# A two-layer decoder trunk: the first norm's weight applied by features, first loads and first product in another order, last stores in pieces

## The chip, the cores and the metric

The kernel runs on one core of a Trainium2 chip. The core has five engines that run side by side and wait for each other by semaphores: TensorE (PE, with its weight loads as PEld), VectorE (DVE), ScalarE (ACT), GpSimd (POOL) and SyncE (SP), which here only starts transfers. The metric is the device time of one execution in microseconds (us), lower is better.

## What is computed

The input is 256 tokens of 1024 features, float32. Two layers follow, cut here to what the change touches:

```
for l in range(2):
    h = rms_norm(x, attn_norm[l])          # x / sqrt(mean(x^2) + eps) * weight
    proj = h @ w_in[l]                     # 1024 -> 1720, cut into 11 parts
    ... two attention groups, mixed, projected by w_out, added to x
    h = rms_norm(x, mlp_norm[l])
    x = x + square(relu(h @ w_ff1[l])) @ w_ff2[l]
return rms_norm(x, final_norm)
```

The weight of the norm belongs to a feature (a column of x), the root of the mean to a token (a row). A product needs h with the features on the partitions, so h is transposed on TensorE first.

## The kernel before

The 256 tokens are two tiles of 128 (t = 0, 1), the 1024 features two halves of 512 (nb = 0, 1), each of four chunks of 128. Float32 products are made of three matmuls: every operand is split into a rounded part `hi` and a rest `lo`, and `mm3` (L350) adds hi·hi, hi·lo and lo·hi (L352 to L354). The factor 1/sqrt(mean) is not applied to h: it is applied to the results, as `rx`, after the product. So the norm before the product (`norm`, L417) is only x times the weight.

Weights come as one stream of tiles `raw` (512 KB, two chunks of 512 columns), which `ask` (L314) starts on SP's queue in the order in which they are used. ACT rounds each to `whi` (L334, two instructions of 512 columns), DVE or POOL subtracts to `wlo` (L336). `raw` has 6 buffers; the first eight tiles go to DVE.

The first norm: `gain` loads the weight onto all 128 partitions (`partition_broadcast`, 256 KB each half), DVE multiplies (L428), TensorE transposes four blocks into the PSUM tile `tr` (two buffers, L384), ACT rounds them in one instruction of 512 columns (L393), DVE subtracts (L394). The order on TensorE and SP is written by the program itself: chains of work (generators) are run by a small planner, `Driver`, that counts expected TensorE time and the times in `dr.event`, and emits the instructions in the order of its clock. ACT, DVE and POOL are ordered by the scheduler of the framework.

The first product (columns 512 to 1023 of w_in) is made by `proj_both` (L851), which takes two chunks of the weights for tile 0 and then for tile 1, four times over. `kcs_after` takes its result to the keys (`kd`, `kcv`), which are transposed later by `key_chain` (started 3468 ns of the planner's clock later). Before data come, TensorE runs matmuls of zeros (`warm_up`, L298). The last norm is `finish` (L1157): after each part of the last sums ACT squares and adds up (`sumsq`, L376), POOL makes the mean (L414) and its power -0.5 (L1164), ACT and DVE scale one half each (L1167, L1169), and each half leaves in one store of 256 KB, ACT's from ACT's queue, DVE's from SP's.

Of the kernel before, what the change touches and what calls it, by code (L numbers as in the profile page):

```python
# [9 lines left out]
F32 = mybir.dt.float32  # L10
# [6 lines left out]
P = 128  # L17
# [131 lines left out]
def _pack(inp):  # L149
# [11 lines left out]
    arr["cst"] = CONSTANTS  # L161
# [65 lines left out]
def trunk(ctx: ExitStack, tc: tile.TileContext, x, wst, gains, pos, cw2, cst, out):  # L227
# [35 lines left out]
    def gain(l, name, halves=()):  # L263
# [3 lines left out]
        if halves:  # L267
            m = n // len(halves)
            for i, also in enumerate(halves):
                nc.sync.dma_start(t[:, i * m : i * m + m], gains[o + i * m : o + i * m + m].partition_broadcast(P))  # L270
                also()
        else:
            nc.sync.dma_start(t, gains[o : o + n].partition_broadcast(P))
        return t

    idt = const.tile([P, P], F32, name="idt")
# [7 lines left out]
    ident = idt  # L284
# [15 lines left out]
    warm_up(9)  # L300
# [109 lines left out]
    def after_x(t, a, n):  # L410

        ss = sumsq(X[t][:, a : a + n], n)
        r = sm.tile([P, 1], F32, name="mean", bufs=6)
        nc.gpsimd.tensor_scalar(r, ss, 1.0 / D, EPS if a == 0 else mean[t], op0=OP.mult, op1=OP.add)  # L414
        mean[t] = r

    def norm(t, nb, g, hT, tag):  # L417

        yield "event", ("x", t, tag, nb * 512)
        if tag[1] == "mlp":  # L420
            if hT[nb] is None:
                hT[nb] = [hl.tile([P, 2, 2, S], F32R, name=f"hm{nb}{i}", tag="hl") for i in range(2)]
        elif hT[nb] is None:
            hT[nb] = halves_pair(f"h{nb}")
        h = tm.tile([P, 512], F32, name="h", tag="tm")
        n = slice(nb * 512, nb * 512 + 512)
# [3 lines left out]
        c = slice(t * P, (t + 1) * P)  # L430
# [40 lines left out]
    def layer(l, hT):  # L471
# [379 lines left out]
        def proj_both(a, chunks, n, after):  # L851

            accs = []
            w = weights(chunks)
            for c in range(0, chunks, 2):
                pairs = [next(w), next(w)]
                for t in range(NT):
                    if c % 4 == 0:
                        yield "event", a(t)[1] + (c // 4,)
                    if c == 0:  # L860
                        yield "get", "s"
                        accs.append(PS("s")[:, :n])
                    h = a(t)[0]
                    for i, wc in enumerate(pairs):
                        mm3(accs[t], h(c + i), wc, c + i == 0, c + i == chunks - 1)
                    yield "pe", 6 * max(107, n / 2.4), 0
                    if c == chunks - 2:
                        after(t, accs[t])
# [14 lines left out]
        def kcs_after(t, acc):  # L883
# [9 lines left out]
            dr.spawn(1, later(3468, key_chain(kd, t, 0, kc)))  # L893
# [250 lines left out]
    def begin(l, halves=()):  # L1144

        g = gain(l, "attn", halves)
# [10 lines left out]
    def finish(t, g):  # L1157
# [7 lines left out]
        for i, h in enumerate(hs):  # L1165
            if i == 0:
# [3 lines left out]
            (nc.sync if i else nc.scalar).dma_start(out[t * P : (t + 1) * P, i * 512 : i * 512 + 512], h)  # L1170

    def main():
        def load_a():
            nc.sync.dma_start(idt, cst[:, :P])
            load_x(1, 0)
            ask(2)

        def load_b():
            load_x(1, 1)
            ask(5)  # L1180

        def next_x():
            load_a()
            load_x(0, 1)

        load_x(0, 0)
        h = begin(0, (next_x, load_b))
        for t in range(NT):
            for nb in range(2):
                dr.event(("x", t, (0, "attn"), nb * 512), [2000, 5000, 2600, 5500][2 * t + nb])  # L1190
# [3 lines left out]
        nc.sync.dma_start(cs, cst)  # L1194
        nc.vector.tensor_copy(identb, ident)
        nc.scalar.copy(maskb, K("causal"))
        yield "event", ("h", 0, (0, "attn"), 0)
        warm_up(4)
# [25 lines left out]
```

## Time and profile before

| what | us |
|---|---|
| timed runs: lowest, median, highest (3 runs) | 634.9, 637.33, 637.53 |
| the profiled execution: its own time | 635.02 |
| the profiled execution: its span, first to last instruction | 633.2 |
| busy in the span: PE, DVE, ACT, POOL | 615.3, 424.0, 354.6, 305.8 |

The profile is of one execution. Busy PE is counted as the union of matmuls that overlap, so a share of 97% is not TensorE at its peak. Outside the span lie 635.02 - 633.2 = 1.8 us. A wait that the profile names is the last that ended before an instruction began.

### The profile page before, as it was taken

To read this page: it belongs to the slowest core of one execution; us is meant where nothing else is said; L and a number is where in the kernel's file an instruction comes from. 1 tells how busy PE (TensorE), PEld (TensorE's weight loads), DVE (VectorE), ACT (ScalarE), POOL (GpSimd) and SP (SyncE) were. 2 spreads that over 40 slices of the span, in tenths; PEclk is the share of its full clock that TensorE was granted. 3 is DMA by queue.
4 is the path that set the end of the run, shared out by engine and by line. 5 is a ranking of instruction groups with operands and counts; after the bars stand their busy time and mean duration, and the time that the engine had idled before them with its cause. 6 is when DMAs were issued, how large, how long until landed. Compare 5 with 4: busy or idle time off the path is not lost.

```text
span 633.2 us, 9990 instructions
## 1 busy us (share of the span) xinstructions
PE 615.3 (97%) x3587; PEld 518.7 (82%) x3587; DVE 424.0 (67%) x742; ACT 354.6 (56%) x776; POOL 305.8 (48%) x292
## 2 busy tenths in 40 slices
PE   8999899999999999999999899999999999999995
PEld 5788788878888888888888778798888888888885
DVE  5997787686647557467677867866774673765662
ACT  5666757555636446365554476665564564454552
POOL 2184415263545636456466641425553654655451
PEclk9999999999999999999999899999999999999999
DMA  8857612245655654755644665116446565565501
GB/s 310 298 187 259 238 45 90 95 155 183 197 170 176 222 167 167 232 167 197 196 128 137 215 215 204 49 53 178 160 139 223 167 216 179 191 210 169 200 1 66
DMA packets 31729, 108.42 MB, mean 171 GB/s; under 512 B 3776, under 2 KB 4416, under 8 KB 31680
## 3 DMA queue, kind: packets, MB, share of 16 engines
q1 hardware_dynamic: 31392, 107.27, 51.6%
q8 instruction: 28, 0.46, 0.3%
q10 hardware_dynamic: 288, 0.52, 0.2%
q14 instruction: 21, 0.17, 0.1%
HBM read 106.73 MB, written 1.05 MB: 170 GB/s over the span
## 4 chain that ended last, share of the span: by engine, by line
PE 83%; DVE 9%; ACT 3%; DMA 2%; issue 2%; POOL 0%; POOLq 0%; SPq 0%; ACTq 0%; DVEq 0%
PE acc L352 14%; PE acc L353 14%; PE acc L354 14%; PE s L1100 14%; PE s L1101 7%; PE pv L1100 5%; PE tr L384 4%; DVE wlo L336 3%; PE pv L1101 2%; PE pv L721 2%; DMA raw<-in_wst_dram 2%; PE pv L772 2%; DVE h L428 1%; PE acc L962 1%; ACT whi L334 1%
## 5 line engine op out<-in xcount | busy, mean ns | idle before, releaser
L336 POOL TENSOR_TENSOR wlo<-raw,whi 128x512 fp32r<-128x512 f32 (+3 forms) x172 | 249.2, 1472 | 208.8 <-ACT whi L334 208.4
L334 ACT CAST whi<-raw 128x512 fp32r<-128x512 f32 (+2 forms) x360 | 201.6, 610 | 96.8 <-PE acc L354 59.6
L336 DVE TENSOR_TENSOR wlo<-raw,whi 128x512 fp32r<-128x512 f32 (+3 forms) x188 | 162.1, 899 | 53.5 <-ACT whi L334 53.5
L1100 PE MATMUL s<-hm,whi 128*128 128x512 f32 x384 | 141.7, 399 | 0.0
L1101 PE MATMUL s<-hm,wlo 128*128 128x256 f32 x384 | 107.8, 281 | 0.0
L352 PE MATMUL acc<-whi,u 128*128 128x512 f32 (+1 forms) x264 | 101.4, 384 | 0.0
L353 PE MATMUL acc<-wlo,u 128*128 128x512 f32 (+1 forms) x264 | 101.1, 383 | 0.0
L354 PE MATMUL acc<-whi,u 128*128 128x512 f32 (+1 forms) x264 | 101.1, 383 | 0.0
L1100 PEld LDWEIGHTS s<-hm,whi 128*128 128x128 f32 x384 | 72.2, 188 | 17.8
L1101 PEld LDWEIGHTS s<-hm,wlo 128*128 128x128 f32 x384 | 72.5, 189 | 0.2
L354 PEld LDWEIGHTS acc<-whi,u 128*128 128x128 f32 x264 | 49.6, 188 | 9.8
L352 PEld LDWEIGHTS acc<-whi,u 128*128 128x128 f32 x264 | 49.6, 188 | 9.8
L353 PEld LDWEIGHTS acc<-wlo,u 128*128 128x128 f32 x264 | 49.6, 188 | 9.4
L1043 DVE SCALAR_TENSOR_TENSOR x<-acc,r,x 128x512 f32<-128x512 f32 (+1 forms) x33 | 24.1, 731 | 49.4 <-PE acc L354 49.4
L1100 PE MATMUL pv<-hm,whi 128*128 128x512 f32 x128 | 51.0, 399 | 0.0
L352 PE MATMUL acc<-whi,h 128*128 128x512 f32 (+2 forms) x112 | 41.3, 369 | 0.0
L353 PE MATMUL acc<-wlo,h 128*128 128x512 f32 (+2 forms) x112 | 40.2, 359 | 0.2 <-POOL wlo L336 0.2
L354 PE MATMUL acc<-whi,h 128*128 128x512 f32 (+2 forms) x112 | 40.0, 357 | 0.0
L1071 ACT COPY sq<-s 128x256 f32<-128x256 f32 x48 | 17.6, 372 | 39.2 <-PE s L1101 38.6
L659 ACT ACTIVATE p<-s,nm 128x128 f32<-128x128 f32 (+1 forms) x96 | 34.0, 433 | 6.5 <-DVE nm L655 3.9
L1076 ACT CAST u<-sq 128x512 fp32r<-128x512 f32 x32 | 19.8, 619 | 31.2 <-DVE sq L1075 31.2
L1101 PE MATMUL pv<-hm,wlo 128*128 128x256 f32 x128 | 36.0, 281 | 0.0
(192 smaller groups left out, 995.7 us busy)
## 6 DMA issues: line engine op xcount, KB each, us to landing
raw<-in_wst_dram SPq DMA_DIRECT2D x178, 512.0 KB, 4.2
raw<-in_wst_dram SPq DMA_DIRECT2D x8, 416.0 KB, 3.6
raw<-in_wst_dram SPq DMA_DIRECT2D x4, 420.0 KB, 5.0
raw<-in_wst_dram SPq DMA_DIRECT2D x4, 384.0 KB, 3.1
x<-in_x_dram SPq DMA_DIRECT2D x4, 256.0 KB, 5.2
g_mix<-in_gains_dram SPq DMA_DIRECT2D x2, 512.0 KB, 5.8
g_mlp<-in_gains_dram SPq DMA_DIRECT2D x2, 512.0 KB, 5.6
g_attn<-in_gains_dram SPq DMA_DIRECT2D x2, 512.0 KB, 4.4
```

The costliest lines, as they stand in the source:

```text
L334: nc.scalar.copy(hi[:, v], r[:, v])
L336: E(eng).tensor_sub(lo[:, v], r[:, v], hi[:, v].bitcast(F32))
L352: mm(acc, ah, wh, start=start, stop=False, **k)
L353: mm(acc, ah, wl, start=False, stop=False, **k)
L354: mm(acc, al, wh, start=False, stop=stop, **k)
L384: nc.tensor.transpose(tr[:rows, c, :], col, ident)
L659: nc.scalar.activation(p[:, k], s[:, k], AF.Exp, bias=nm[:, a : a + 1], scale=scale)
L1043: nc.vector.scalar_tensor_tensor(X[t][:, c], acc, scale, X[t][:, c], op0=OP.mult, op1=OP.add)
L1071: nc.scalar.copy(low[:, n], acc[:, S:])
L1076: nc.scalar.copy(hi, sq)
L1100: mm(accs[half][j], wh[:, f], h.rearrange("p k n -> p (k n)"), start=c == 0, stop=False)
L1101: mm(accs[half][j][:, :S], wl[:, f], h[:, 0], start=False, stop=c == KC - 1)
```

## The change

The first norm's weight now comes as eight columns beside the identity matrix (feature on the partition, chunk on the column): the constants get a field `gain0`, and one load brings both. The x tiles are transposed as they are; the weight is applied when ACT and DVE take the transposed blocks from PSUM, one instruction for each block of 128, since each block has its own column of the weight. The first loads stand in another order, `proj_both` takes four chunks for a tile before it turns to the other tile, seven and two matmuls of zeros stand where nine and four stood, and the key chains of the first layer start 5500 ns after their product. At the end tile 1 is scaled and stored in four pieces, and the mean of the parts under 512 columns is made by DVE.

```diff
     add("ident", np.eye(P))
+    add("gain0", np.zeros((P, KC)))
...
+    arr["cst"][:, a : a + n] = inp["attn_norm"][0].reshape(KC, P).T
...
-    idt = const.tile([P, P], F32, name="idt")
+    idg = const.tile([P, P + KC], F32, name="idt")
...
-    warm_up(9)
+    warm_up(7)
...
-        nc.gpsimd.tensor_scalar(r, ss, 1.0 / D, EPS if a == 0 else mean[t], op0=OP.mult, op1=OP.add)
+        (nc.vector if n < 512 else nc.gpsimd).tensor_scalar(r, ss, 1.0 / D, EPS if a == 0 else mean[t], op0=OP.mult, op1=OP.add)
...
+        if g is None:
+
+            tr = yield from trans([X[t][:, n][:, j * P : (j + 1) * P] for j in range(4)])
+            hi, lo = (x[:, :, c] for x in hT[nb])
+            gf = idg[:, P + nb * 4 : P + nb * 4 + 4]
+            with urgent():
+                for j in range(4):
+                    nc.scalar.activation(hi[:, j], tr[:, j], AF.Copy, scale=gf[:, j : j + 1])
+                for j in range(4):
+                    nc.vector.scalar_tensor_tensor(lo[:, j], tr[:, j], gf[:, j : j + 1], hi[:, j].bitcast(F32), op0=OP.mult, op1=OP.subtract)
...
-            for c in range(0, chunks, 2):
-                pairs = [next(w), next(w)]
-                for t in range(NT):
+            for t, part in [(0, (0, 4)), (1, (0, 4)), (0, (4, 8)), (1, (4, 8))]:
...
-            dr.spawn(1, later(3468, key_chain(kd, t, 0, kc)))
+            dr.spawn(1, later(3468 if l else 5500, key_chain(kd, t, 0, kc)))
...
-        for i, h in enumerate(hs):
-            if i == 0:
+        for a in range(0, D, 256 if t else 512):
+            n = 256 if t else 512
+            h = hs[a // 512][:, a % 512 : a % 512 + n]
+            if a < 512:
                 nc.scalar.activation(h, h, AF.Copy, scale=v)
             else:
                 nc.vector.tensor_scalar(h, h, v, None, op0=OP.mult)
-            (nc.sync if i else nc.scalar).dma_start(out[t * P : (t + 1) * P, i * 512 : i * 512 + 512], h)
+            (nc.sync if a >= 512 else nc.scalar).dma_start(out[t * P : (t + 1) * P, a : a + n], h)
...
         load_x(0, 0)
-        h = begin(0, (next_x, load_b))
+        nc.sync.dma_start(idg, cst[:, : P + KC])
+        ask(1)
+        load_x(1, 0)
+        ask(2)
+        load_x(0, 1)
+        load_x(1, 1)
+        ask(5)
+        h = begin(0)
...
-        warm_up(4)
```

What stands on SP's queue at the start before: x of tile 0 first half, weight of the norm first half, identity, x of tile 1 first half, two weight tiles, x of tile 0 second half, weight of the norm second half, x of tile 1 second half, three weight tiles. After: x of tile 0, identity with the weight, a weight tile, x of tile 1, a weight tile, x of tile 0 and x of tile 1 second halves, three weight tiles.

TensorE's queue at the start of the program before the change; `h` is x times the weight, `whi_127` the first weight tile, `s_227` and `s_234` the sums of tile 0 and tile 1, and each name of a tile has its buffer number:

```order
L384 MATMUL tr_197<-idt_96,h_193 128x128 x4
L384 MATMUL tr_204<-idt_96,h_195 128x128 x4
L298 LDWEIGHTS zero_102
L298 MATMUL s_211<-zero_102 128x512
...
L352 MATMUL s_227<-whi_127,h00_191 128x512
L353 MATMUL s_227<-wlo_128,h00_191 128x512
L354 MATMUL s_227<-whi_127,h01_192 128x512
...
L352 MATMUL s_234<-whi_127,h00_191 128x512
```

After the change; `x0_94` and `x1_95` are x of tile 0 and 1, `tr_219` is tile 1's first half, `tr_234` tile 0's second, `tr_264` tile 1's second, `s_215` and `s_277` are the sums:

```order
L381 MATMUL tr_166<-idt_96,x0_94 128x128 x4
...
L349 MATMUL s_215<-whi_122,h00_164 128x512
L350 MATMUL s_215<-wlo_123,h00_164 128x512
L351 MATMUL s_215<-whi_122,h01_165 128x512
L381 MATMUL tr_219<-idt_96,x1_95 128x128 x4
L381 MATMUL tr_234<-idt_96,x0_94 128x128 x4
L349 MATMUL s_215<-whi_122,h00_164 128x512
...
L351 MATMUL s_215<-whi_131,h01_165 128x512
L381 MATMUL tr_264<-idt_96,x1_95 128x128 x4
L349 MATMUL s_277<-whi_122,h00_164 128x512
```

Only tile 0's first transposes stand before the first product now; the other three groups have moved in among its matmuls, and tile 1 begins after tile 0's four chunks.

ACT's queue at the start before the change; `junk` is the square for the mean, `h00` and `h10` the rounded halves:

```order
L376 ACTIVATE junk_169,ss_168<-x0_94 128x512
L376 ACTIVATE junk_174,ss_173<-x1_95 128x512
L393 CAST h00_191<-tr_197 128x4x128
L393 CAST h00_191<-tr_204 128x4x128
L334 CAST whi_127<-raw_125 128x512 x2
L334 CAST whi_135<-raw_133 128x512 x2
```

The same place after the change:

```order
L373 ACTIVATE junk_183,ss_182<-x0_94 128x512
L331 CAST whi_122<-raw_120 128x512 x2
L431 ACTIVATE h00_164<-tr_166,idt_96 128x128 x4
L373 ACTIVATE junk_188,ss_187<-x1_95 128x512
L331 CAST whi_131<-raw_129 128x512 x2
L373 ACTIVATE junk_193,ss_192<-x0_94 128x512
L431 ACTIVATE h00_164<-tr_219,idt_96 128x128 x4
L431 ACTIVATE h10_232<-tr_234,idt_96 128x128 x4
```

The first weight tile has moved ahead of the first half of h, and each half of h and tile is four instructions where it was one.

ACT's last instructions, of tile 1, before the change:

```order
L376 ACTIVATE junk_6785,ss_6784<-x1_95 128x256
L1167 ACTIVATE h_5123<-h_5123,rstd_6790 128x512
L1170 DMA out_0_dram<-h_5123 128x512
```

and after it:

```order
L373 ACTIVATE junk_6794,ss_6793<-x1_95 128x256
L1177 ACTIVATE h_5132<-h_5132,rstd_6799 128x256 x2
L1180 DMA out_0_dram<-h_5132 128x256 x2
```

Both scalings stand ahead of both stores.

## Rows read from the trace of the kernel before

**Rows 1.** Windows of first and second product: us, busy PE PEld DVE ACT POOL, clock, DMA

```profile
9.47:23.08 13.61, 12.84 (x57) 9.76 (x57) 11.67 (x22) 10.83 (x23) 3.94 (x6) 1.00 1.03 398
23.08:35.62 12.54, 12.29 (x58) 9.60 (x57) 12.40 (x28) 6.73 (x18) 5.17 (x5) 1.00 0.67 219
```

**Rows 2.** Chain of waits, first 15 us: start, us, what

```profile
1.16 4.09 DMA g_attn<-in_gains_dram
6.10 2.19 PE tr L384 x8
14.23 0.23 PE s L354
```

**Rows 3.** Timeline: start, us, engine, line, operation, count; the second product's first matmul

```profile
23.08 0.39 PE L352 MATMUL acc<-whi,h 128*128 128x512 f32 x1
```

**Rows 4.** DMA view, single issues at 0.72, 1.63, 2.10, 2.57: KB, us to landing

```profile
x<-in_x_dram SPq DMA_DIRECT2D x1, 256.0 KB, 2.7
idt<-in_cst_dram SPq DMA_DIRECT2D x1, 64.0 KB, 4.0
x<-in_x_dram SPq DMA_DIRECT2D x1, 256.0 KB, 4.3
raw<-in_wst_dram SPq DMA_DIRECT2D x1, 512.0 KB, 5.1
```

**Rows 5.** DMA view, 0 to 30 us in 40 slices

```profile
GB/s 0 0 128 369 154 129 277 412 371 410 399 391 240 298 415 415 432 420 419 407 405 392 421 415 389 407 384 395 394 406 407 365 265 262 275 111 244 218 22 0
```

**Rows 6.** Timeline of ACT and DVE, 11 to 31 us: casts, square, instructions of 128 columns

```profile
11.80 0.63 ACT L376 ACTIVATE junk<-x 128x512 bf16<-128x512 f32 x1 [0.20 <-DMA x<-in_x_dram]
13.02 1.14 ACT L334 CAST whi<-raw 128x512 fp32r<-128x512 f32 x2 [0.49 <-DMA raw<-in_wst_dram]
29.36 0.34 DVE L459 SCALAR_TENSOR_TENSOR ra<-s,rx,cs 128x128 f32<-128x128 f32 x1
29.62 0.46 DVE L462 SCALAR_TENSOR_TENSOR rb<-s,rx,cs 128x64 f32<-128x64 f32 x2
30.18 0.37 ACT L881 ACTIVATE kcv<-s,rx 128x128 f32<-128x128 f32 x1 [3.67 <-DVE rb L462]
30.44 0.36 ACT L881 ACTIVATE V<-s,rx 128x128 f32<-128x128 f32 x1
```

**Rows 7.** Groups by line, 3 to 24 us: count, busy us, mean ns, idle before

```profile
L393 ACT CAST h<-tr 128x512 fp32r<-128x512 f32 x4 | 2.3, 586 | 1.3 <-PE tr L384 1.3
```

**Rows 8.** View of line 298, the matmuls of zeros: duration ns min/median/max

```profile
L298 PE MATMUL s<-zero x13: 380/634/634, 1.0 to 9.3; 128*128 128x512 bf16 x13
```

**Rows 9.** Windows and timeline at 355 us, second layer

```profile
355.00:360.00 5.00, 2.90 (x10) 2.79 (x11) 3.81 (x11) 3.07 (x9) 1.35 (x4) 0.74 0.89 323
357.10 0.45 PE L384 MATMUL tr<-idt,kd 128*128 128x128 f32 x2 [2.27 <-DVE kT L509]
```

**Rows 10.** Timeline of POOL and PE at 46 to 55 us

```profile
46.07 1.39 POOL L528 TENSOR_TENSOR FT<-kcT,posl 64x120 f32<-64x120 f32 x2
54.48 0.65 PE L962 MATMUL acc<-raw,FT 128*32 128x128 f32 x16
```

**Rows 11.** Timeline of the end, and a small DVE instruction from 61 us

```profile
627.29 0.42 ACT L376 ACTIVATE junk<-x 128x256 bf16<-128x256 f32 x1 [1.97 <-DVE x L1043]
627.96 0.27 POOL L414 TENSOR_SCALAR mean<-ss,mean 128x1 f32<-128x1 f32 x1 [2.27 <-ACT junk L376]
628.31 0.55 POOL L1164 TENSOR_TENSOR rstd<-mean,mhalf 128x1 f32<-128x1 f32 x1
628.89 0.72 ACT L1167 ACTIVATE h<-h,rstd 128x512 f32<-128x512 f32 x1 [1.10 <-POOL rstd L1164]
629.65 0.34 ACTq L1170 DMA_DIRECT2D out_dram<-h  x1
61.29 0.18 DVE L732 RECIPROCAL wv<-pv 128x4 f32<-128x4 f32 x1
```

**Rows 12.** DMA view, last store: KB, us to landing

```profile
out_dram<-h ACTq DMA_DIRECT2D x1, 256.0 KB, 2.5
```

More of the change, by code (lines that the diff above doesn't have):

```diff
@@ L160, in _pack @@
     arr["cw2"] = np.concatenate([w2k, w2v.reshape(L, P, 128)], 2)
-    arr["cst"] = CONSTANTS
+    arr["cst"] = CONSTANTS.copy()
+    a, n = CST["gain0"]
+    arr["cst"][:, a : a + n] = inp["attn_norm"][0].reshape(KC, P).T
     return {k: np.ascontiguousarray(v) for k, v in arr.items()}
@@ L261, in trunk, with gain @@
     goff = {"attn": (0, 1024), "mix": (1024, 1024), "mlp": (2048, 1024), "lat": (3072, 384)}
-    def gain(l, name, halves=()):
+    def gain(l, name):
         o, n = goff[name] if l < L else (0, 1024)
@@ L266, in gain @@
         t = gp.tile([P, n], F32, name=f"g_{name}", tag="glat" if name == "lat" else "g", bufs=1 if name == "lat" else 2)
[L267 to L273, printed above, removed]
+        nc.sync.dma_start(t, gains[o : o + n].partition_broadcast(P))
         return t
-    idt = const.tile([P, P], F32, name="idt")
+    idg = const.tile([P, P + KC], F32, name="idt")
     cs = const.tile([P, cst.shape[1]], F32, name="cs")
@@ L283, in trunk @@
     ck = lambda name, t, n: K(name)[:, t * n : (t + 1) * n]
-    ident = idt
+    ident = idg[:, :P]
     identb = const.tile([P, P], BF16, name="identb")
@@ L424, in norm @@
             hT[nb] = halves_pair(f"h{nb}")
+        n = slice(nb * 512, nb * 512 + 512)
+        c = slice(t * P, (t + 1) * P)
+        if g is None:
[7 more added lines that the diff above has]
+                    nc.vector.scalar_tensor_tensor(lo[:, j], tr[:, j], gf[:, j : j + 1], hi[:, j].bitcast(F32), op0=OP.mult, op1=OP.subtract)
+            dr.put("tr", 1500)
+            dr.event(("h", t, tag, nb), 1600)
+            return
         h = tm.tile([P, 512], F32, name="h", tag="tm")
-        n = slice(nb * 512, nb * 512 + 512)
         with urgent():
@@ L429, in norm @@
         yield "pe", 0, 700
-        c = slice(t * P, (t + 1) * P)
         cols = [h[:, j * P : (j + 1) * P] for j in range(4)]
@@ L851, in proj_both @@
         def proj_both(a, chunks, n, after):
-            accs = []
-            w = weights(chunks)
-            for c in range(0, chunks, 2):
-                pairs = [next(w), next(w)]
-                for t in range(NT):
[L858 to L868, printed above, removed]
+            src, w, accs = weights(chunks), [], [None, None]
+            for t, part in [(0, (0, 4)), (1, (0, 4)), (0, (4, 8)), (1, (4, 8))]:
+                yield "event", a(t)[1] + (part[0] // 4,)
+                if part[0] == 0:
+                    yield "get", "s"
+                    accs[t] = PS("s")[:, :n]
+                h = a(t)[0]
+                for c in range(*part):
+                    if c == len(w):
+                        w.append(next(src))
+                    mm3(accs[t], h(c), w[c], c == 0, c == chunks - 1)
+                    yield "pe", 3 * max(107, n / 2.4), 0
+                if part[1] == chunks:
+                    after(t, accs[t])
         hin = lambda t: (of_tile(hT, t), ("h", t, tag("attn")))
@@ L1142, in layer, with begin @@
         return hN
-    def begin(l, halves=()):
-        g = gain(l, "attn", halves)
+    def begin(l):
+        g = gain(l, "attn") if l else None
         h = [None, None]
@@ L1169, in finish @@
                 nc.vector.tensor_scalar(h, h, v, None, op0=OP.mult)
-            (nc.sync if i else nc.scalar).dma_start(out[t * P : (t + 1) * P, i * 512 : i * 512 + 512], h)
+            (nc.sync if a >= 512 else nc.scalar).dma_start(out[t * P : (t + 1) * P, a : a + n], h)
     def main():
[L1173 to L1184, printed above, removed]
-        load_x(0, 0)
-        h = begin(0, (next_x, load_b))
+        load_x(0, 0)
+        nc.sync.dma_start(idg, cst[:, : P + KC])
[6 more added lines that the diff above has]
+        h = begin(0)
         for t in range(NT):
             for nb in range(2):
-                dr.event(("x", t, (0, "attn"), nb * 512), [2000, 5000, 2600, 5500][2 * t + nb])
+                dr.event(("x", t, (0, "attn"), nb * 512), [1900, 4300, 3900, 4700][2 * t + nb])
+        nc.sync.dma_start(cs, cst)
+        yield "event", ("h", 0, (0, "attn"), 0)
+        warm_up(2)
         for nb in range(2):
@@ L1193, in main @@
                 after_x(t, nb * 512, 512)
-        nc.sync.dma_start(cs, cst)
         nc.vector.tensor_copy(identb, ident)
         nc.scalar.copy(maskb, K("causal"))
-        yield "event", ("h", 0, (0, "attn"), 0)
-        warm_up(4)
         for l in range(L):
```

## The prediction

> **What bounds the kernel now.** I read the windows by stage first, then the chain of waits at the start, the transfers, and the timeline at both ends. TensorE is the engine that sets the pace: in the first product it is busy 12.84 of 13.61 us, in the second 12.29 of 12.54, while DVE (12.40 of 12.54) runs close behind it in the second [rows 1]. The second product's first matmul starts at 23.08 us [rows 3], and from there TensorE hardly stops for long, so a time won before 23.08 should reach the end of the program if nothing else holds it back. What holds the start is in the chain [rows 2]: a transfer of the norm's weight that lands at 1.16 + 4.09 = 5.25, DVE's multiplication, eight transposes from 6.10 to 8.28, ACT's and DVE's split, and only then, at 9.47, the first real matmul [rows 1]. In 9.47 to 23.08 the 48 matmuls at 0.23 us each [rows 2] make 11.0 us; the other 2.6 are transposes and waits. The edits at the start act on these 23 us, those at the end on the last 6; on the other engines the order in between is nearly untouched.
>
> **The transfers.** x's first half lands at 0.72 + 2.7 = 3.4, the weight of the norm at 5.25, the identity at 1.63 + 4.0 = 5.6, the next x at 6.4, the first weight tile at 2.57 + 5.1 = 7.7 [rows 2, 4]. They land in the order of issue, so 512 KB take 7.67 - 6.40 = 1.27 us, half of it for 256 KB. The weight of the norm took 5.25 - 3.4 = 1.8 us for 256 KB, and while it came the rate fell to 154 and 129 GB/s, against about 400 later [rows 5]. With it gone and the identity next (0.4 us, as from 5.25 to 5.6), I place the landings at 3.8 for identity and gain, 5.1 for the first weight tile, 5.8 for x of tile 1, 7.0 for the second weight tile, 7.7 and 8.3 for the second halves of x, 9.6 and 10.9 for the next weight tiles. The other end: if the low rate is that of a start, and not of this load, everything lands 1.3 later.
>
> **The small instructions.** Removed are four multiplications on DVE, four casts on ACT of 0.59 us [rows 7] and four subtractions on DVE. Added are 16 ACTIVATE and 16 SCALAR_TENSOR_TENSOR of 128 columns. The nearest rows, with a scale from a column too, last 0.37 on ACT and 0.34 on DVE, but the next one starts 0.26 later on both [rows 6]. I take 0.26 each and 0.37 for the last, so 1.15 for a group of four; the other end is 0.37 each, 1.5. The Trainium skill's page "ScalarE: Activation LUTs", section "What ACT_TABLE_LOAD costs", speaks against cutting: an ACTIVATE has 186 ns of its own, 93 more for a scale taken from a column, and neighbours overlap by 93, which gives 293 ns at 128 columns as an estimate against the 260 of the row. By the page the eight that stand on the path below would cost 0.3 us more and the sum would be 632.7; the row decides for me.
>
> **The path to the end of the first product.** ACT works in order, and the new order puts the first weight tile ahead of tile 0's h, so all that follows waits for the landing at 5.1: two casts of the first weight tile, 1.14 [rows 6], from 5.1 to 6.3; four for tile 0's h to 7.4; a square with its readout, about 0.75, to 8.1; two casts of the second tile to 9.2; a square to 9.9; four for tile 1 to 11.0, four for tile 0's second half to 12.1. DVE follows: tile 0's rest 7.2 to 8.3, the second weight tile's rest to about 10.1, tile 1's rest 10.3 to 11.4. TensorE's first real matmul goes at 6.7, when the first rounded block is there. The third waits for DVE to 7.5. Eight transposes stand behind it in the queue; at the 0.27 of the early ones (2.19 for eight [rows 2]) they end near 9.8. All else of TensorE is queued behind them, tile 0's remaining nine matmuls first, and these need the second weight tile's rest anyway (10.1). They end near 12.0. The last four transposes need DVE to have read `tr_219` (11.4), so they wait for nothing more and end at 12.5. Then 36 matmuls at 0.23 make 8.3: the product ends at 20.8, against 23.08. The next weight tiles (9.6, 10.9, cast by 15) are in time. This edit gives 2.3 us. Early end: transposes twice as fast and no wait, 19.6, a gain of 3.5. Late end: the transfers 1.3 later and 8 x 0.11 for the instructions, 23.0, no gain.
>
> **The middle.** The second stage needs 48 x 0.23 = 11.0 us and eight transposes; 1.5 of its 12.54 us are not matmuls [rows 1]. The key chains, started later in the planner's order, should spare some waits; I take 0.2, from 0.6 gained to 0.5 lost, since DVE has 0.14 us free there and must now run 2.3 us earlier. POOL's last additions to `FT` move back in its queue behind two more weight halves, but they end at 47.5 and are wanted at 54.48 [rows 10], so 7 us cover that. The zero matmuls lie in TensorE's waiting time.
>
> **The end.** The mean moves from POOL (0.27) to DVE, where the smallest row is 0.18; I take 0.15 gained with the handover, from -0.2 to 0.3 [rows 11]. Two scalings of 256 columns on ACT, each up to 0.42 where the one took 0.72, cost 0.06 to 0.12. Both stores stand behind both scalings, so the second is issued one issue of 0.34 later, but carries 128 KB less, about 0.33 us. The last store lands 2.5 us after its issue [rows 12]. Together 0.1 gained, from 0.5 lost to 0.5 gained. The Trainium skill's page "DMA: Bandwidth & Descriptors", section "Anatomy of one DMA — SWDGE (gpsimd) path", has a rule against more and smaller stores: about 2.0 us of a transfer are fixed and only bytes/436e3 scale. By it, halving saves 0.30, less than the second issue costs, and the end would come out even. The last store's 2.5 us [rows 12] agree with the 2.6 that the page gives for 256 KB, as an estimate.
>
> **The sum.** 2.3 + 0.2 + 0.1 = 2.6. Against the profiled execution's 635.02 that is 632.4. The timed runs are 634.9, 637.33 and 637.53, so the profiled one lies with the lowest, 2.3 below the median. Nothing in the change shows which level the median of new runs takes: 632.4 or 637.33 - 2.6 = 634.7. I take the middle, 633.5.
>
> **Rivals.**
> 1. TensorE's clock eats part of it. The zero matmuls took 634 ns at first and 380 at the last [rows 8], that is 1.2 GHz and then 2.4, after near continuous work from 6.1. At 355 us the granted clock of the stretch is 0.74, after an idle time of 2.27 us [rows 9]. Now TensorE's early work is broken by waits between 6 and 12 us. If the rise comes only a quarter into the dense 36 matmuls, nine of them last 0.2 longer (512 columns at 1.2 in place of 2.4 GHz), 1.8: a gain of 0.8, 634.2 on the profiled level, 636.5 on the median's. For: fewer zero matmuls. Against: five unbroken us from 0.97. Chance 0.2.
> 2. The removed load wasn't what slowed the transfers, and the landings stay 1.3 later: gain 1.3, so 633.7 or 636.0. For: only one such stretch at the very start. Against: the rate falls again (240, 298) when the second half of that weight comes [rows 5]. Chance 0.1.
> 3. Slower: the clock stays at 1.2 GHz through the whole first product, because TensorE never gets a stretch without a wait. Each 512-column matmul then costs 0.2 more; 48 make 9.6, so 635.02 - 2.6 + 9.6 = 642.0. It decides from 13 matmuls on against no gain, from 29 on against 0.5% slower. Against: after 12 us, 36 matmuls stand without a wait between them. Chance 0.06.
> 4. More than forecast: 3.5 at the start and 0.6 in the middle, 630.9 to 633. Chance 0.1.
>
> **How the numbers follow.** The forecast has 0.54. About 0.5% (3.2 us) is what a measurement of this kernel can tell from no change. Against the median of 637.33, faster means below 634.1: some two thirds of the forecast's chance (0.37), nearly all of rival 4 (0.1), a little of rivals 1 and 2 (0.05): 0.52. Slower by more than 3.2 is rival 3: 0.06. The rest, 0.42, is within. The range goes from 630.5 (rival 4 on the lower level) to 637.0 (rivals 1 and 2 on the upper level, with some loss in the middle); the forecast's own is 632.0 to 635.2.
>
> **What would show it.** Right: the first weight tile lands near 5.1, the first real matmul starts near 6.7, the second product's first near 20.8, and every stage after it lies 2 to 3 us earlier with the same lengths. Wrong: a landing after 6; matmuls of 512 columns 0.43 apart after 12 us; a second product longer than 12.5; the last store landing more than 4.9 us after the last square starts (629.65 + 2.5 - 627.29 before [rows 11, 12]). The forecast fails most easily if the second stage gives back what the first won.

## The result, and the profile after

The changed kernel takes 631.92 us (median of 18 runs, 630.1 to 636.7) against 634.9 (18 runs, 632.93 to 640.42). The ratio is 0.995, with a 95% interval of 0.9927 to 0.9974: 3.2 us faster, 1.7 to 4.6, just at the half per cent that this kernel's measurement can tell from no change. The forecast was 633.5, its sum a gain of 2.6. The profiled executions differ by 2.4: own time 632.59 and span 630.8 us, against 635.02 and 633.2.

I paired TensorE's instructions of the two traces in program order and subtracted their start times. This is where the 2.4 us lie, beside what the prediction had put there:

| stretch (us in the kernel before) | forecast | profiled pair |
|---|---|---|
| start to the second product's first matmul, 23.1 | 2.3 | 0.29 |
| 23 to 60, second and third product | 0.2 | 0.57 |
| 60 to 350 | 0 | 0.68 |
| 357 to 361, TensorE at 1.2 GHz in the kernel before alone | 0 | 1.55 |
| 373 to 378, a wait of TensorE for DVE | 0 | -0.83 |
| 378 to 620 | 0 | 0.10 |
| the end | 0.1 | 0.03 |

So the sum was nearly right and its terms were not. Of the 0.68 in 60 to 350 us, 0.38 lie in 138 to 164 us, and they are the program's: the ten traces of the changed kernel and its variants have 0.37 to 0.39 there (after_quiet counted against before_quiet), the other variants of the kernel before have none. In 430 to 480 us of the second layer eight of the ten gain 0.39 to 0.44 as well; this pair has 0.05. Which edit makes it is open.

The views below are of the changed kernel: the stretches of the first and the second product (columns as in [rows 1]), TensorE's timeline (start, us, engine, line, operation, tiles, count, idle time before and its releaser), ACT's and DVE's, and the DMA rate from 0 to 30 us in 40 slices.

```profile
8.18:22.79 14.61, 14.18 (x60) 11.58 (x61) 13.35 (x34) 14.11 (x38) 2.30 (x7) 0.88 1.01 384
22.79:34.39 11.60, 11.60 (x56) 9.57 (x55) 10.34 (x24) 5.67 (x16) 4.74 (x4) 1.00 0.71 217
```

```profile
4.79 1.06 PE L295 MATMUL s<-zero 128*128 128x512 bf16 x2
8.18 0.50 PE L349 MATMUL s<-whi,h 128*128 128x512 f32 x1 [2.34 <-ACT h L431]
9.34 0.80 PE L351 MATMUL s<-whi,h 128*128 128x512 f32 x1 [0.43 <-DVE h L433]
9.93 1.91 PE L381 MATMUL tr<-idt,x 128*128 128x128 f32 x8
22.79 0.39 PE L349 MATMUL acc<-whi,h 128*128 128x512 f32 x1
```

```profile
6.72 1.14 ACT L331 CAST whi<-raw 128x512 fp32r<-128x512 f32 x2 [2.65 <-DMA raw<-in_wst_dram]
7.77 1.13 ACT L431 ACTIVATE h<-tr,idt 128x128 fp32r<-128x128 f32 x4
8.94 1.13 DVE L433 SCALAR_TENSOR_TENSOR h<-tr,idt,h 128x128 fp32r<-128x128 f32 x4 [0.27 <-ACT h L431]
```

```profile
GB/s 0 0 164 270 194 339 276 270 311 391 363 380 401 410 421 437 391 385 419 395 426 421 428 371 402 405 390 375 300 192 354 208 146 302 135 195 266 146 281 345
```

The first weight tile lands at 6.7, not 5.1: the rate stays under 340 GB/s until 7 us, where [rows 5] had reached 412 after the load of the norm's weight. It comes 3.2 us behind the identity (3.50), where the forecast had 1.3. ACT waits 2.65 us for it and TensorE 2.34. From there the chain is the forecast one: the groups of four small instructions last 1.13 (1.15 forecast), the first real matmul comes 1.46 after the landing (1.6), the third 1.16 later (0.8). But TensorE's clock is at half from 9.1 to 12.5 us, behind the wait (it was granted in full from 5.7; the two matmuls of zeros just before, 1.06 us, still ran at 1.2 GHz): the granted clock of the product is 0.88, and eight transposes take 1.91 (2.19 in [rows 2], the size that the forecast had used). The product starts 1.29 earlier and lasts 1.0 longer than in [rows 1].

The second product is TensorE's alone now (busy 11.60 of 11.60, DVE 10.34), 0.94 shorter than in [rows 1]; part of that are transposes that moved behind it. 0.56 of it are two waits that the kernel before has and this one has not. Before, two pairs of key-chain transposes start 0.55 and 0.47 us after the matmul ahead of them (31.49 to 32.04, 34.17 to 34.64), where 0.23 is the usual distance. The second pair waits for DVE to read `tr` (L509, to 34.58), which stands behind a `qr` of 1.57 us that started just after a subtraction of weights on POOL. In the changed kernel `qr` starts before POOL's, takes 0.69, and no transposes wait there. The kernel before (POOL, DVE, TensorE), then the changed one (DVE, POOL):

```profile
32.57 2.61 POOL L336 TENSOR_TENSOR wlo<-raw,whi 128x416 fp32r<-128x416 f32 x2 [3.93 <-ACT whi L334]
32.68 1.57 DVE L468 TENSOR_TENSOR qr<-ra,rb 128x512 f32<-128x512 f32 x1
34.64 0.44 PE L384 MATMUL tr<-idt,kcv 128*128 128x128 f32 x2
```

```profile
31.38 0.69 DVE L478 TENSOR_TENSOR qr<-ra,rb 128x512 f32<-128x512 f32 x1
31.82 2.24 POOL L333 TENSOR_TENSOR wlo<-raw,whi 128x416 fp32r<-128x416 f32 x2 [4.14 <-ACT whi L331]
```

The end, in the changed kernel, answering [rows 11] and [rows 12]: ACT's last square, DVE's mean, POOL's root, the two scalings, the two issues on ACT's queue, and the landing of both.

```profile
624.92 0.42 ACT L373 ACTIVATE junk<-x 128x256 bf16<-128x256 f32 x1 [1.97 <-DVE x L1051]
625.47 0.21 DVE L411 TENSOR_SCALAR mean<-ss,mean 128x1 f32<-128x1 f32 x1 [0.18 <-ACT junk L373]
625.76 0.55 POOL L1172 TENSOR_TENSOR rstd<-mean,mhalf 128x1 f32<-128x1 f32 x1 [4.52 <-DVE mean L411]
626.34 0.91 ACT L1177 ACTIVATE h<-h,rstd 128x256 f32<-128x256 f32 x2 [0.91 <-POOL rstd L1172]
626.88 0.82 ACTq L1180 DMA_DIRECT2D out_dram<-h  x2
out_dram<-h ACTq DMA_DIRECT2D x2, 128.0 KB, 2.2
```

From the last square to the end of the span it is 5.88 us (630.8 - 624.92) against 5.91 (633.2 - 627.29): even, where 0.1 was forecast. The mean comes 0.18 sooner to POOL's root (0.84 after the square against 1.02), the scalings 0.18 sooner (1.42 against 1.60); the second issue takes it back.

In the second layer a product of 128x4 numbers on DVE decides a wait. The kernel before (POOL, DVE, TensorE), then the changed one:

```profile
376.73 2.51 POOL L336 TENSOR_TENSOR wlo<-raw,whi 128x512 fp32r<-128x512 f32 x2 [0.68 <-ACT whi L334]
376.71 0.16 DVE L733 TENSOR_TENSOR wv<-wv,gates 128x4 f32<-128x4 f32 x1
377.48 0.52 PE L721 MATMUL pv<-V,pt 128*128 128x65 f32 x3 [0.65 <-DVE otmp L735]
```

```profile
373.37 2.49 POOL L333 TENSOR_TENSOR wlo<-raw,whi 128x512 fp32r<-128x512 f32 x2 [0.41 <-ACT whi L331]
373.63 1.03 DVE L743 TENSOR_TENSOR wv<-wv,gates 128x4 f32<-128x4 f32 x1
375.26 0.52 PE L731 MATMUL pv<-V,pt 128*128 128x65 f32 x3 [1.77 <-DVE otmp L745]
```

Before, DVE started 0.02 us ahead of POOL's subtraction of a weight half and took 0.16. Now POOL starts 0.26 ahead, DVE takes 1.03, and TensorE waits 1.77 in place of 0.65.

### The profile page after: what moved, and what is told of

Same layout as the page of the kernel before. It is cut to its first block, busy times and chain, and to the rows that moved or that the text cites. A ratio compares the mean times of both kernels' runs of the same rounds, so it can differ in the third digit from the quotient of the medians.

```text
span 630.8 us, 10001 instructions
## 1 busy us (share of the span) xinstructions
PE 610.8 (97%) x3583; PEld 517.8 (82%) x3583; DVE 424.1 (67%) x753; ACT 357.0 (57%) x789; POOL 303.3 (48%) x290
## 4 chain that ended last, share of the span: by engine, by line
PE 80%; DVE 10%; ACT 4%; issue 2%; DMA 2%; POOL 0%; SPq 0%; POOLq 0%; ACTq 0%
PE s L1108 14%; PE acc L349 13%; PE acc L351 13%; PE acc L350 13%; PE s L1109 7%; PE pv L1108 5%; PE tr L381 4%; DVE wlo L333 3%; DMA raw<-in_wst_dram 2%; PE pv L1109 2%; PE pv L731 2%; PE pv L782 2%; ACT whi L331 1%; PE acc L970 1%; DVE h L439 1%
## 5 line engine op out<-in xcount | busy, mean ns | idle before, releaser
L349 PE MATMUL acc<-whi,h 128*128 128x512 f32 (+2 forms) x112 | 40.5, 362 | 0.0
L351 PE MATMUL acc<-whi,h 128*128 128x512 f32 (+2 forms) x112 | 39.4, 352 | 0.0
```

The costliest lines, as they stand in the source:

```text
L349: mm(acc, ah, wh, start=start, stop=False, **k)
L351: mm(acc, al, wh, start=False, stop=stop, **k)
```

## The experiments

### Undoing one part at a time

My first theory (A): the gain comes after the first product, from key-chain transposes that no longer hold up TensorE's queue; the first product is bound by the late weight tile and the low clock. Four kernels ran together.

**chain_alone**, the kernel before with this alone:

```
-            dr.spawn(1, later(3468, key_chain(kd, t, 0, kc)))
+            dr.spawn(1, later(3468 if l else 5500, key_chain(kd, t, 0, kc)))
```

> The kernel before with one edit alone: in layer 0 the key chains are due 5500 later instead of 3468. Theory A (the changed kernel's gain was made after the first product, by key-chain transposes that no longer hold up TensorE's queue): the second product's first matmul stays at 23.08 us, and by 70 us TensorE's instructions lie 0.8 us earlier than in the kernel before (they lay 1.05 earlier in the changed kernel, 0.29 of which it had at the start of the second product); median 0.8 us lower. Theory B (the transposes only move and cost the same further on; the gain is the start and the clock): 0.0 at 70 us, no change of the median.

Measured: 641.58 us against 635.41, ratio 1.0095 (1.0061 to 1.0129). It is slower by 6, and at 70 us TensorE lies 3.6 later; most of the rest is a wait of 1.79 at 382 us and the clock's fall behind it (below). Both theories fall.

**chain_undone**, the changed kernel with that line as it was before:

> The changed kernel with the key chains of layer 0 due at 3468 again. Theory A: the second product starts at 22.79 us as in the changed kernel, but by 70 us TensorE's instructions lie 0.3 us earlier than in the kernel before instead of 1.05; median 0.8 us above the changed kernel's, near 632.7. Theory B: 1.05 earlier at 70 us as well, median 631.9.

Measured: 634.86 against 635.41, ratio 0.9994 (0.9972 to 1.0017); at 70 us 1.1 to 1.2 later than the kernel before. Counted from the second product's start to 70 us, the later due time is worth 1.8 us in the changed kernel's profile; in the kernel before it costs 3.8. On the medians it is worth 1 to 3 (634.86 against 633.88 and 631.92, not measured together) and costs 6. Without it TensorE waits 0.38 for POOL and 1.11 for DVE at 46 and 48 us. The gain of 0.7 from the second product's start to 36 us is there without it too. The second product of chain_undone starts at 23.11, though the work up to there is the changed kernel's (22.79): from 8.2 to 13.4 us its matmuls start 0.43 us apart or more, as at 1.2 GHz, where the changed kernel's profile has the low clock from 9.1 to 12.5.

**turns_undone**, the changed kernel with the old `proj_both` (two chunks of both tiles in turn):

> The changed kernel with the first product's old order (two chunks of tile 0, two of tile 1, in turn), all else as changed. Theory A (the first product is held by the late first weight tile, by TensorE's low clock from 9.1 to 12.5 us and by the number of its matmuls, not by their order): the second product's first matmul within 0.3 us of 22.79. Theory C (with pairs TensorE waits for tile 1's rest on DVE, ready near 13.3 us, with six matmuls done): 13.3 + 42 x 0.23 + four transposes = 23.4 us, 0.6 later than changed; that would make the order of chunks worth more than the whole 0.29 won at the start.

Measured: 641.93, ratio 1.0091 (1.0073 to 1.011); the second product starts at 25.52. Theory C had the direction and too small a size: TensorE waits 1.54 before 14.09 for tile 1's rest, and the product takes 17.92 us. The clock column of that window reads 1.00, but the rows don't bear it out: matmuls start 0.43 us apart until 16.7 and 0.23 after, so TensorE ran at 1.2 GHz until then (one row of either kind).

```profile
16.28 0.63 PE L349 MATMUL s<-whi,h 128*128 128x512 f32 x1
17.33 0.39 PE L349 MATMUL s<-whi,h 128*128 128x512 f32 x1
```

At 70 us it lies 4.0 behind the kernel before; most of the rest is the second layer's wait and clock, as in chain_alone. Against chain_undone, whose clock is low from the start as well, the old order costs 2.4 (25.52 - 23.11): the wait, and some 0.9, as an estimate, of a clock that stays low 3.3 us longer.

**zeros12**, the changed kernel with TensorE kept at work through its wait:

```
-        warm_up(2)
+        warm_up(12)
```

> The changed kernel with 12 zero matmuls instead of 2 behind the first four transposes, so that TensorE works through its wait of 2.34 us for the first weight tile. Theory A (the wait let TensorE's clock fall to 1.2 GHz from 9.1 to 12.5 us, which slowed eight transposes and five matmuls): eight transposes 1.1 us instead of 1.91, matmuls 0.23 apart from 8.2 us on, second product's first matmul near 22.0 instead of 22.79, median 0.8 lower, 631.1. Theory D (the clock doesn't matter there because TensorE then waits for DVE's rests: tile 1's at 13.3, the last at 18.1 us): second product's first matmul at 22.6 or later, median unchanged. If the clock is still low when the zeros run, ten more cost 4.3 us and the first real matmul comes at 9.9 instead of 8.18.

Measured: 636.51, ratio 1.0027 (0.9999 to 1.0054). At the start theory A holds. In TensorE's timeline the eight transposes take 1.09, and the first product (window of its own) lasts 13.91 at full clock:

```profile
4.67 2.75 PE L295 MATMUL s<-zero 128*128 128x512 bf16 x12
8.23 0.50 PE L349 MATMUL s<-whi,h 128*128 128x512 f32 x1 [0.81 <-ACT h L431]
9.73 1.09 PE L381 MATMUL tr<-idt,x 128*128 128x128 f32 x8
8.23:22.14 13.91, 12.93 (x61) 10.20 (x61) 12.24 (x32) 13.70 (x38) 2.31 (x7) 1.00 1.03 399
```

So the fall of the clock costs the start 0.70 us (14.61 - 13.91); in chain_undone, where it is low until 13.4, 1.40 (15.31 - 13.91). But the 0.65 won is lost and 2.1 more by 70 us (expectations below say 1.8). In DVE's timeline of this kernel and in POOL's, ahead of TensorE's next wait (2.56 us at 47.37):

```profile
46.10 3.02 POOL L333 TENSOR_TENSOR wlo<-raw,whi 128x512 fp32r<-128x512 f32 x2
45.63 2.37 DVE L333 TENSOR_TENSOR wlo<-raw,whi 128x384 fp32r<-128x384 f32 x2
47.92 1.23 DVE L920 TENSOR_SCALAR gates<-gates 128x24 f32<-128x24 f32 x1
49.19 0.69 DVE L553 TENSOR_TENSOR qT<-tr,qT 64x512 fp32r<-64x512 f32 x1
```

In the changed kernel the first two of DVE's lie beside POOL's additions to `FT` and TensorE waits 0.26:

```profile
44.75 1.54 DVE L333 TENSOR_TENSOR wlo<-raw,whi 128x384 fp32r<-128x384 f32 x2
46.21 0.43 DVE L920 TENSOR_SCALAR gates<-gates 128x24 f32<-128x24 f32 x1
44.02 2.58 POOL L538 TENSOR_TENSOR FT<-kcT,posl 64x120 f32<-64x120 f32 x4
46.67 2.53 POOL L333 TENSOR_TENSOR wlo<-raw,whi 128x512 fp32r<-128x512 f32 x2
```

This gave theory E: DVE paces 23 to 50 us, and an instruction of it with two SBUF inputs is held up by some 0.9 us when it starts beside a subtraction of weights on POOL. The Trainium skill's page "SBUF — State Buffer", section "Who interferes with whom", states this as a rule: DVE's second input from SBUF goes through a read interface shared with GpSimd, the one that comes first keeps it, and a GpSimd instruction that only writes doesn't contend. The traces agree: 0.16 against 1.03 for the 128x4 product above, by who came first.

### Taking POOL's subtractions away, and the load put back

In layer 0 POOL writes zeros in place of its subtractions: before_quiet is the kernel before with this edit, after_quiet the changed kernel, chain_quiet chain_alone.

```
+                    if eng == "g" and at_w[1] <= len(PLAN) // L:
+                        nc.gpsimd.memset(lo[:, v].bitcast(F32), 0.0)
+                    else:
+                        E(eng).tensor_sub(lo[:, v], r[:, v], hi[:, v].bitcast(F32))
```

The "excess" is the sum, over DVE's instructions that start in 23 to 50 us, of the duration less the shortest of the same line and shape in any trace.

> The kernel before, with the rests of the weights that POOL computes in layer 0 left out (zeros written in their place, so part of the weights' precision is missing). Theory E (DVE's instructions with two SBUF inputs, 0.58 to 0.69 us alone, take 1.4 to 1.6 when they start beside POOL's subtractions of weights, and DVE paces 23 to 50 us): the excess of DVE's instructions over their shortest like falls from 6.6 us to under 2.5 in 23 to 50 us, and TensorE's instructions at 70 us come 1 us or more earlier than in the kernel before. Theory F (what counts is where the key-chain transposes stand in TensorE's queue): as the kernel before, within 0.3.

> The changed kernel with the same left out (POOL's rests of layer 0, zeros in their place). Theory E: the 0.76 us that the changed kernel gained between the second product's start and 70 us were collisions it happened to miss, so against the kernel before with the same left out only the 0.29 of the start remain, 0.0 to 0.5 at 70 us. Theory F: 1.05 earlier at 70 us as between the full kernels.

> The kernel before with the key chains of layer 0 due at 5500, and POOL's rests of layer 0 left out (zeros in their place). With the rests this order lay 3.6 us behind the kernel before at 70 us. Theory E (POOL then does its subtractions of weights at 32 to 37 us, beside DVE's, six of which take 1.3 to 1.6 us there): the 3.6 us vanish, within 0.7 of the kernel before with the rests left out. Theory F: still 3 us behind it.

Measured (one run each): the excess falls from 6.7, 5.4 and 7.4 to 1.9, 1.9 and 1.8. The kernel before gains 1.0 us by 60 and 2.1 by 70. Between the two quiet kernels (before, after) the stretch from the second product's start to 60 us differs by 0.09, where it was 0.57; at 70 us 0.26 remains. In before_quiet the two pairs of transposes stand where they stood and start 0.23 after the matmul ahead (31.65 and 33.95). So the changed kernel's gain in 23 to 60 us was in meetings missed: theory E. That POOL itself is done sooner is no rival for it: in the kernel before TensorE waits for POOL nowhere from 23 to 60 us. The excess is a sign and not a price: the changed kernel's second execution, below, has 6.8 and the same gain by 60. Of chain_alone's 3.6 us 2.6 are gone; 1.0 stays (1.5 counted from the second product's start), with a wait of 1.84 at 42.69 for DVE, so the order by itself costs something too, as theory F had it, and "within 0.7" was missed. DVE and POOL in chain_alone, then in chain_quiet:

```profile
31.82 4.47 DVE L336 TENSOR_TENSOR wlo<-raw,whi 128x280 fp32r<-128x280 f32 x4
36.22 1.56 DVE L468 TENSOR_TENSOR qr<-ra,rb 128x512 f32<-128x512 f32 x1
31.96 2.49 POOL L336 TENSOR_TENSOR wlo<-raw,whi 128x416 fp32r<-128x416 f32 x2 [3.46 <-ACT whi L334]
34.68 2.55 POOL L336 TENSOR_TENSOR wlo<-raw,whi 128x416 fp32r<-128x416 f32 x2 [0.23 <-ACT whi L334]
```

```profile
32.85 1.10 DVE L339 TENSOR_TENSOR wlo<-raw,whi 128x416 fp32r<-128x416 f32 x2 [2.02 <-ACT whi L334]
33.86 0.69 DVE L471 TENSOR_TENSOR qr<-ra,rb 128x512 f32<-128x512 f32 x1
33.39 0.83 POOL L337 MEMSET wlo<- 128x416 f32 x2 [1.88 <-PE acc L356]
```

`qr` takes 1.56 beside POOL's subtraction and 0.69 beside its memset, which reads nothing. Four halves of weights (two of 280 columns and two of 416) take 4.47 in the one; the two of 416 take 1.10 in the other.

**load_back**:

```
+        unused = at.tile([P, 512], F32, name="unused")
+        nc.sync.dma_start(unused, gains[:512].partition_broadcast(P))
         nc.sync.dma_start(idg, cst[:, : P + KC])
```

> The changed kernel with a broadcast load of the norm's weight (first half, 256 KB into SBUF) put back between x and the identity; nothing reads it. Theory G (the prediction's: that load takes 1.8 us of the transfers' time where its bytes would take 0.6): the first weight tile lands 1.3 to 1.8 us later than 6.7, at 8.0 to 8.5. Theory H (the transfers are slow in the first microseconds whatever they are; the load counts by its bytes at the start's 270 GB/s): 1 us later, 7.5 to 7.8. If it lands within 0.3 of 6.7 the removal was worth nothing.

Measured: the first weight tile lands at 8.0, the second product starts at 24.35 (636.67 us, one run). That is 1.3 later than in the first profile, as theory G had it, and 1.3 to 2.6 later than in the eight traces that load x, identity and the whole tile without it (5.4 to 6.75); 0.47 of it is that the tile is issued later (2.10 against 1.63). So the load did hold the tile back; one run doesn't fix by how much. The first step of the prediction was right in the direction of the difference, and wrong in the level from which it counted.

### Once more, and the small product

> The changed kernel once more, word for word. It shows what differs between two executions of one program: if the second product's first matmul, 22.79 us in the first profile, moves by 0.3 (kernels with the same work up to there had 23.11 and 23.12), the 0.29 won at the start is no gain at all; if it stays within 0.1, it is one. For 70 us I expect 1.0 us earlier than the kernel before, give or take 0.4, and TensorE's waits of 1.75 us at 65 and 1.77 at 373 us for DVE again, since the order of DVE and POOL there is a matter of 0.2 us; whether the clock falls after the second may differ. Median 631.9.

Measured: 633.88 against 634.77, ratio 0.9976 (0.9946 to 1.0006): by itself this doesn't tell the changed kernel from the one before. ACT's first cast, TensorE's first real matmul and the second product's first in this trace:

```profile
5.41 1.14 ACT L331 CAST whi<-raw 128x512 fp32r<-128x512 f32 x2 [1.29 <-DMA raw<-in_wst_dram]
6.86 0.61 PE L349 MATMUL s<-whi,h 128*128 128x512 f32 x1 [2.01 <-ACT h L431]
21.50 0.39 PE L349 MATMUL acc<-whi,h 128*128 128x512 f32 x1
6.86:21.50 14.64, 14.45 (x61) 11.07 (x61) 12.66 (x32) 13.21 (x36) 2.30 (x7) 0.88 1.02 399
```

The same program now has its first weight tile at 5.4, near the 5.1 of the forecast, and starts the second product at 21.50. The 1.3 us of the landing go through one to one: TensorE's instructions from 19 to 62 us lie 1.29 ahead of the first profile's, within 0.04. Five traces of this code up to there have the second product at 21.50, 22.72, 22.79, 23.11 and 23.12; four of the kernel before's have 22.51, 22.94, 23.01 and 23.08. The start's gain is thus about 0.2 on the mean, and its size differs from one execution to the next by more than that. Landing and clock make the difference: counted from ACT's first cast, the five take 16.09, 16.40, 16.07, 16.77 and 16.72, and the last two are chain_undone and after_quiet, whose matmuls start 0.43 apart until 13.4 us. What follows to 60 us is the program's and repeats; at 65 us it does not, with a wait of 1.75 in the one execution and 0.39 in the other. My 0.1 and 0.3 were both far too narrow.

**after_wv**, the same number of instructions; the product's one input is in PSUM, so only one is in SBUF (`inverse` is one plus the exponential, of which `gates` is the reciprocal; the lines that make it are left out):

```
-                nc.vector.reciprocal(wv, o[:, :, :, DK])
-                nc.vector.tensor_mul(wv, wv, gates[t][:, heads, 1:3])
+                nc.vector.tensor_mul(wv, o[:, :, :, DK], inverse[t][:, heads, 1:3])
+                nc.vector.reciprocal(wv, wv)
```

> The changed kernel, with the attention's small weights computed in another order: first the sum times the gate's inverse (the sum is in PSUM, so the product has one SBUF input), then the reciprocal, as many instructions as now. Theory E (a product of two SBUF inputs on 128x4 numbers, 0.16 us alone, takes 1.03 where POOL's subtraction of weights starts just before it, and TensorE waits for it): that product takes under 0.3 us everywhere, TensorE's wait at 65 us falls from 1.75 to 0.6 or less and that at 373 from 1.77 to 0.65, and the clock does not fall in the 7 us after it; 2.2 us at least, median 629.7 or lower. Theory I (the next thing in line, ACT's exponentials or DVE's maximum, is as late, and the wait only moves): under 0.5 us, median 631.5.

Measured: 631.12 (629.89 to 632.93), ratio 0.9936 (0.991 to 0.9961); against the 633.88 of the changed kernel, measured beside it, it is 2.8 lower on the medians, though the two intervals overlap a little. The waits are 0.69 at 65 and 0.58 at 374, as theory E had them, and theory I falls. The median missed 629.7. DVE and TensorE in this trace:

```profile
374.00 0.15 DVE L742 TENSOR_TENSOR wv<-pv,inverse 128x4 f32<-128x4 f32 x1
374.96 1.08 PE L731 MATMUL pv<-V,pt 128*128 128x65 f32 x8 [0.58 <-DVE otmp L745]
```

The wait has a second price. Windows of the stretch behind it (us, TensorE's busy time, granted clock, DMA share, GB/s) in the changed kernel, in its second execution, in chain_alone and in after_wv:

```profile
375.30:382.00 6.70, 6.70 (x73) 1.00 0.69 245
373.60:380.40 6.80, 6.80 (x58) 0.75 0.54 188
382.30:388.90 6.60, 6.60 (x42) 0.50 0.39 145
375.00:381.80 6.80, 6.79 (x73) 1.00 0.74 257
```

Six of the fourteen profiled executions had this wait at 1.75 to 1.80 us, and in five of them TensorE ran at 1.2 GHz behind it, for half or all of the next 6.8 us; it cost 1.66 us in the second of these windows, over 3 in the third. In the eight with a wait of 0.65 or less it never did. In the first layer the like wait, 1.75 to 1.79 at 65 to 67 us, was followed by it in one of four. At 351 to 359 us all fourteen wait 2.3 us, and nine fell, the kernel before's first profile among them, the changed kernel's two not: that is the 1.55 us of the table. Of the ten traces with the changed first loads five fell, of the four with the old ones all four; so the change does not prevent it, and whether it makes it rarer these counts don't show.

### Winning the start as well

**wv_half6**: after_wv, the first weight tile in two halves, and `warm_up(6)` (of the edit, the loop that loads the halves):

```
+            for a in range(0, m, m // 2) if at_w[1] == 1 else [0]:
+                b = a + m // 2 if at_w[1] == 1 else m
+                nc.sync.dma_start(r[:, a:b], src[:, a:b])
```

> The kernel of the run before (the attention's small weights in another order) with the first weight tile loaded in two halves and 6 zero matmuls instead of 2 behind the first transposes. At the start: the first half should land 0.8 us before the whole did (6.7), so ACT begins near 5.9, the first real matmul comes near 7.4 instead of 8.18, the clock stays at 2.4 GHz, and the second product starts 0.9 to 1.3 us earlier, near 21.8. Theory J (what is won at the start reaches the end): median 0.9 us or more below the same kernel without it. Theory E says that this is open: DVE's and POOL's instructions meet anew between 23 and 50 us, at 0.9 us for each meeting, so anything from 1.5 lost to 1.5 gained; with 12 zero matmuls the start won 0.65 and 70 us was reached 1.8 later.

Measured: 631.59, ratio 0.9954 (0.9926 to 0.9981). The first half is there at 4.97, the second only at 7.77, and TensorE waits for ACT, which casts both before it turns to tile 0's h; the second product starts at 23.83. The clock did not stay up either: it is at 0.50 from 11.1 to 14.5 us. The start is worse, the total no different.

**wv_zeros12**: after_wv with `warm_up(12)`.

> The kernel with the attention's small weights in another order, and 12 zero matmuls instead of 2 behind the first transposes. At the start the clock should stay at 2.4 GHz through the wait for the first weight tile, whenever that lands: with a landing at 6.7 the second product began 0.65 earlier (22.14 against 22.79), with one at 5.4 it should begin near 20.9 against 21.50. Theory J (the start's gain reaches the end): median 0.7 to 1.5 below the 631.12 of the same kernel with 2. Theory E (DVE and POOL meet anew between 23 and 50 us, 0.9 a meeting; with 12 zero matmuls and the old order of the small weights 70 us was reached 1.8 later): median 630 to 633, no gain to be counted on.

Measured: 635.93, ratio 1.002 (0.9998 to 1.0042). The second product starts at 21.67, 1.1 earlier than in the first profile, and from 46 to 52 us all of it and 3.6 more are lost: POOL's subtraction at 45.63, DVE's weights 2.38 in place of 1.54, `inverse` 1.23, and a wait of 2.55 on TensorE, with its clock down behind it. From 20 to 46 us this trace is that of zeros12, 0.47 earlier throughout, with the same meetings: they are no chance but part of the program. Theory J falls. Theory E had that no gain is to be counted on, but not a loss of this size: 635.93 lies outside its 630 to 633.

## Why the prediction was right, and where it was not

- **The transfers** are the step that failed. "I place the landings at 3.8 for identity and gain, 5.1 for the first weight tile": identity and gain came at 3.5, the weight tile at 6.7 in the profiled execution and at 5.4 in the second. The tile took 3.2 and 1.8 us behind the identity, where the sum had 1.3, the distance of two later landings. That the removed load had held it back was right (load_back, one run: 1.3 to 2.6), that the transfers run at the later rate without it was not. The prediction's late end of this term (1.3 later, 23.0, no gain) is close to the profiled start; rival 2 had the landing, with a gain of 1.3 for it.
- **The path to the end of the first product** nearly holds, counted from the landing: 15.7 us forecast (20.8 - 5.1), 16.07 and 16.09 measured (22.79 - 6.72, 21.50 - 5.41), and 16.4 to 16.8 in the three other traces. The clock's fall behind TensorE's wait costs 0.70, up to 1.4 where it was low for longer, but the forecast had its transposes at the slow size already. Rival 1 had the mechanism, with 1.8 for it; rival 3 did not come.
- **The new order of chunks** was no term of its own. With the new loads it is worth 2.4 us (25.52 - 23.11), 1.54 of it a wait.
- **The small instructions** were right: 1.13 for four against 1.15, 2.18 for eight.
- **The middle**, 0.2, was mis-sized: 0.57 by 60 us. Two waits of 0.56 us in all are spared, but "The key chains, started later in the planner's order, should spare some waits" is not the reason: chain_undone, without the later start, is rid of them too. They were there because of a `qr` that met POOL's subtraction, and without POOL's subtractions the difference is nearly gone (0.09). The later start spares other waits beside the other edits (1.11 and 0.38 in chain_undone), and alone it costs 3.8 us by 70 us. "POOL's last additions to `FT`... 7 us cover that" looked at who waits for them, not at what runs beside them.
- **The end**, 0.1 forecast, 0.03 measured: the step held, nearer to even. The section of the Trainium skill's page "DMA: Bandwidth & Descriptors" that the prediction cites there is on transfers by GpSimd's path, and these stores leave on ACT's queue; the rows agree with its 0.30 for half the bytes all the same (2.5 and 2.2 us to landing).
- **Nothing was set for what lies behind 60 us**: 0.38 in 138 to 164 us, which repeats in every trace, and in the second layer 1.55 of falling clock on one side and 0.83 of a DVE wait on the other.
- **The level**: 633.5 is the middle between two levels of the kernel before, from three runs with a median of 637.33. Eighteen runs have 634.9, so the lower level held, and the sum from there is 632.3 (634.9 - 2.6).

That the time fell in the range, and near the forecast, is therefore partly luck: 2.3 at the start became 0.2 to 1.6, and 23 to 350 us gave 1.25 where 0.2 was forecast. What repeats is less: some 0.2 at the start on the mean, 0.57 to 60 us, 0.38 in 138 to 164 us. There matmuls of 512 columns average 393 ns in the changed kernel and 401 in the kernel before (groups by line); the cause stays open, as does that of the low rate of the transfers in the first 7 us.

## What to carry to other kernels

Where DVE paces a stage and GpSimd works beside it, look at each DVE instruction with two SBUF inputs for its longest and its shortest case: a part that starts earlier may turn one into the other. Give a small instruction on the path one input from PSUM, as after_wv does, and the question is gone. A gain at the start is worth what the next stage lets through, so read an edit's worth with the others in place and then alone: here one line was worth 1.8 us by 70 us or cost 3.8.

## What was not expected of the hardware

- One DVE product of 128x4 numbers takes 0.16 us or 1.03, by which of two engines started first, 0.02 us ahead or 0.26 behind.
- The same wait of TensorE is not always followed by half clock: of 1.75 to 1.80 us five of six times at one place and one of four at another, of 2.3 us nine of fourteen. Twelve zero matmuls ahead of the first product kept the clock at 1.00 through it, in two kernels of two; six did not, in one of one.
- The landing of the first weight tile differs by 1.3 us between two executions of one program (5.4 and 6.7), and everything to 62 us moves with it.
